# Two-layer hybrid encoder trunk: the residual in DRAM during the mixers, and the value products of a scan step after the step before it

## The chip, the cores and the metric

The kernel runs on one core of one Trainium2 chip. The metric is the device time of one execution in microseconds (us). Matrix products run on TensorE (PE, with its weight loads as PEld), elementwise work on VectorE (DVE) and ScalarE (ACT); nearly all transfers are issued on the queue of SyncE (SP). GpSimd (POOL) only clears a few edges.

## What is computed

Two layers and a final RMS norm over 256 tokens of width 1024, in float32. The inner widths are 2816 (feed-forward) and 8 heads of 64 (mixers).

```python
for l in range(DEPTH):
    x = x + 0.5 * gt1 * swiglu(modulate(rmsnorm(x), sh1, sc1), wi[l, 0], wo[l, 0])
    h = modulate(rmsnorm(x), sh2, sc2)
    x = x + gt2 * hybrid_mixer(h)
    x = x + 0.5 * gt3 * swiglu(modulate(rmsnorm(x), sh3, sc3), wi[l, 1], wo[l, 1])
return rmsnorm(x, final_norm)

def hybrid_mixer(h):
    proj = h @ w_in
    o_a = dilated_attention(...)            # mixer A
    o_b = neighborhood_attention(...)       # mixer B
    o_c = rwkv7_bidirectional(...)          # mixer C, a scan over the tokens
    return (sigmoid(gz0) * (o_a @ P_a) + sigmoid(gz1) * (o_b @ P_b)
            + sigmoid(gz2) * (o_c @ P_c)) @ w_out

def _rwkv_step(state, inp):
    r, w, k, v, a_vec, b_vec = inp
    sa = einsum("dbhvk,dbhk->dbhv", state, a_vec)
    state = state * w[..., None, :] + sa[..., None] * b_vec[..., None, :] + v[..., None] * k[..., None, :]
    return state, einsum("dbhvk,dbhk->dbhv", state, r)
```

The shifts, scales and gates (`sh`, `sc`, `gt`) are nine products of the conditioning vector with `ada_w` per layer.

## The kernel before

Activations lie transposed, 128 channels by 256 tokens a tile. Every weight product is done in three matmuls on two fp32r halves of weight and activation (lines 404 to 406, `mm3`): these are the **dense** matmuls. Weights stream as 512 KB tiles `wraw` (three buffers, line 345); ACT casts a high half `whi` (line 360) and DVE subtracts it for the low half `wlo` (line 369).

**The planner.** The order of the instructions on each engine is fixed when the kernel is built. The code is written as threads (generators). `Order.run` steps the thread that can start first by a table of durations, and writes its instructions down. The thread `main` yields the dense products; the rest are spawned beside it. Memory is a counted resource: `take(s_big)` and `free_big` count the pool of big tiles (`big`, 4 KB per partition, `NBIG` buffers), `take(s_z)` the pool of small ones (`small`, `NZ`), `take(s_px)` and `take(s_pm)` the eight PSUM banks. A thread that finds no buffer stands still, and so does everything after it in that thread.

**The residual** `xT` (128 x 8 x 256) is a tile of its own that is held through the whole kernel. In a mixer it is read at the start (`modulated`, which makes the normed input `h`) and not again until `residual` adds the mixer's output.

**A mixer** (`mixer`, from line 853) runs its dense work by `ORDER = "cabAgB"`: projections for C, A and B, then the gates and branch product of A (`join(0)`), the gates of C (`gates2`, which takes two big tiles `sg2` first), `join(1)`, and last the branch product of C (`branch(2)`), which needs the finished scan, and `w_out`. 480 dense matmuls stand between the start of `gates2` and the branch product of C.

**The scan of C** goes over four chunks of 64 tokens, both directions at once. Chunk `n` needs:

- `invert` (line 1142, two threads that take the chunks in turn, at most `NCK` = 2 chunks in hand): products `pG`, masks on DVE, a block inverse in `blocks8` (one PE product `p` at line 1228, then a row of short DVE operations), and three doubling levels, each with a product `pX` (line 1181), a copy, a product `pT` (line 1193), a masked copy and a transpose (`flip`, line 1245) on DVE. The result is `TT`.
- `values` (line 1247): transposes `pBT` (line 1258), products `pvt` (line 1267) and `pMV` (line 1277) with their copies; they depend on the chunk but not on the state. The results are `bu`, `uv` and `W1`.
- `scan` (line 1285): `pAS`, `pU`, `pS`, `pY` in a row, each after the copy of the one before, from the state of chunk `n - 1`.

Before the change `invert` takes all tiles of a chunk at once, those of `values` too:

```python
for _ in range(5 - (n == 3) + (n == ns[0])):
    yield take(s_big)
```

`post` normalizes the scan's output (products `pvar` and `pgi`, line 1402 and 1420) and writes `oC`, the input of the last branch product. Beside all this, `ada` reads the `ada_w` blocks (`araw`, 512 KB each, line 495) and reduces each on DVE (line 468) with the lowest priority; every one needs a big tile too.

Of the kernel before, what the change touches and what calls it, by code (L numbers as in the profile page):

```python
# [21 lines left out]
BIG = 1e30  # L22
TWO_PI_PARTS = (6.28125, 0.0019350051879882812, 3.0199159819e-07)
ROUND = 12582912.0
NBIG, NZ, NZ2 = 34, 10, 2
NRAW, NSPL, NADA, NPM = 3, 4, 2, 3
ORDER = "cabAgB"
NCK, NLR = 2, 2
WARM = 0
NJ0 = 8  # L30
NXF, NXM = 4, 8
# [130 lines left out]
def wait(ev):  # L162
    return ("wait", ev, 0, 0)
# [28 lines left out]
def trunk(ctx, tc, A, out):  # L192
# [36 lines left out]
        eng.dma_start(t, A[key])  # L229
        return t  # L230

    xT = act.tile([128, KT, S], F32, name="xT")
    csb = const.tile([128, D], F32, name="csb")
    cT = cload("cT", [128, KT], eng=nc.sync)
    ident = cload("ident", [128, 128], eng=nc.sync)
# [393 lines left out]
    def modulated(l, n, st, ha):  # L629
        yield from rstd(st)  # L630
        yield wait(st.e_A)
        for k in range(KT):
            yield take(s_z)
            t = small("ht")
            yield on("DVE", 0.4)
            V.scalar_tensor_tensor(t, xT[:, k], st.Ac[:, k:k + 1], st.r, op0=OP.mult, op1=OP.mult)
            od.spawn(mod_put(l, n, k, t, ha), 1)
        st.used()
# [214 lines left out]
    def mixer(l, st):  # L853
        yield take(s_big, 4)
        ha = Act("h", KT)
        od.spawn(modulated(l, 1, st, ha), 0)
        vec = tmp.tile([128, 14, 4], F32, name="vec", bufs=1)
        mul = tmp.tile([128, 2], F32, name="mul", bufs=1)
        for t, src in ((vec[:, 0:13], "vec"), (mul, "mul")):
# [262 lines left out]

        e_inv, e_val = ([Event() for _ in range(4)] for _ in range(2))
        CH = {}
        s_ck = Sem(NCK)
        n_inv, e_got = [0], [Event() for _ in range(5)]

        def toks(c):
            return slice(c * 64, c * 64 + 64)
# [1 line left out]
        def invert(ns):  # L1131
            for e in e_ab:
                yield wait(e)
            for n in ns:
                cs = (n, 3 - n)
                if n > 0:
                    yield wait(e_got[n - 1])
                yield take(s_ck)
                for _ in range(5 - (n == 3) + (n == ns[0])):
                    yield take(s_big)  # L1140
                od.set(e_got[n])
                if n == ns[0]:
                    tx = big("tx", (128, 2, 2, 4, 64))
                    T, X = tx[:, 0], tx[:, 1]
                G = [big("G", (128, 2, 4, 128)) for _ in range(2)]
                uv = big("uv", (128, 2, 8, 64))
                bu = big("bu", (128, 2, 8, 64)) if n < 3 else None
                tw = big("tw", (128, 2, 2, 4, 64))
                TT, W1 = tw[:, 0], tw[:, 1]
                for d in range(2):  # L1150
                    yield take(s_px, 2)
                    pp = [paux("pG", (128, 4, 128)) for _ in range(2)]
                    yield on("PE", 1.3)
                    for i in range(4):
                        for b in range(2):
                            hs = half(b)
                            P.matmul(pp[b][:, i], BK[d][i // 2][hs, i % 2, cs[d]].rearrange("p a b -> p (a b)"),
                                     ar_view(d, i // 2)[hs, :, i % 2, toks(cs[d])], start=True, stop=True)
                    for b in range(2):
                        yield on("DVE", 0.6)  # L1160
                        V.tensor_mul(G[b][:, d], pp[b], mg[:, d][:, None, :].to_broadcast([128, 4, 128]))
                        od.release(s_px)
                yield from blocks8(G, X, TT)
                yield on("DVE", 0.6)
                flip(T, TT)
                od.spawn(values(n, cs, G, bu, uv, W1), VPRIO)
                for lv in range(3):
                    w = 8 << lv

                    def part_(t, d, a):  # L1170
                        return t[:, d].rearrange("p h c -> p (h c)").rearrange("p (x a s) -> p x a s", a=2, s=w)[:, :, a]

                    def halves_(t, a):
                        return skew(part_(t, 0, a), part_(t, 1, 1 - a))

                    yield take(s_px)
                    px = paux("pX", (128, 2, 4, 64))
                    yield on("PE", 0.85)
                    for d in range(2):
                        for h in range(8):  # L1180
                            P.matmul(px[half(h), d, h // 2], G[h % 2][half(h), d, h // 2, 0:64], T[half(h), d, h // 2],  # L1181
                                     start=True, stop=True)
                    if lv == 0:
                        yield from copy_any(X, px, 512)
                    else:
                        yield from copy_any(halves_(X, 0), halves_(px, 0), 256)
                    od.release(s_px)
                    yield take(s_px)
                    pt = paux("pT", (128, 2, 4, 64))
                    yield on("PE", 0.85)  # L1190
                    for d in range(2):
                        for h in range(8):
                            P.matmul(pt[half(h), d, h // 2], X[half(h), d, h // 2], TT[half(h), d, h // 2], start=True, stop=True)  # L1193
                    yield on("DVE", 0.335)
                    V.copy_predicated(halves_(TT, 1), lvl[:, lv].rearrange("p d (x s) -> p d x s", s=w), halves_(pt, 1))
                    od.release(s_px)
                    if lv < 2:
                        yield on("DVE", 0.6)
                        flip(T, TT)
                CH[n] = (G, bu, uv, TT, W1)  # L1200
                yield wait(e_val[n])
                od.set(e_inv[n])
            n_inv[0] += 1
            free_big(1 if n_inv[0] == 1 else 5)

        def blocks8(G, m, TT):

# [36 lines left out]

            V.transpose(t.rearrange("p d a b -> p (d a b)"), tt.rearrange("p d a b -> p (d a b)"))

        def values(n, cs, G, bu, uv, W1):
            for d in range(2):
                yield wait(e_rkv[d, 2])
            if n < 3:  # L1250
                yield take(s_px, 2)
                p = [paux("pBT", (128, 2, 4, 64)) for _ in range(2)]
# [26 lines left out]
            yield from copy_any(W1, p, 512)  # L1279
            od.release(s_px)  # L1280
            od.set(e_val[n])

        e_y = {(d, t): Event() for d in range(2) for t in range(2)}

        def scan():
# [2 lines left out]
            yield take(s_big)  # L1288
            for n in range(4):
                cs = (n, 3 - n)  # L1290
                yield wait(e_inv[n])
                G, bu, uv, TT, W1 = CH[n]
                ar = lambda d, h, z: ar_view(d, h // 4)[half(h), z, h // 2 % 2, toks(cs[d])]
# [52 lines left out]
                od.release(s_px)  # L1346
                free_big(5 - (n == 3))
                od.release(s_ck)
                ST = sn
            free_big(5)  # L1350

# [382 lines left out]
        ha.free()  # L1734
        yield take(s_big, 4)
        ma = Act("m", KT)
        yield wait(e_oC)
        yield from branch(2, oC[0], gts)
        free_big(4)
# [2 lines left out]
        yield wait(have[l, 5])  # L1742
        yield on("DVE", 0.07)
        V.tensor_scalar(g, mod(l, 5), 0.5, None, op0=OP.mult)
        p3 = []
        for m in range(NPM):
            yield take(s_pm)
# [23 lines left out]
    def main():  # L1771
# [14 lines left out]
        for k in range(KT):  # L1786
            yield on("DVE", 0.34)
            V.tensor_mul(xT[:, k], xT[:, k], st.r)
            if k % 2 == 0 or k == KT - 1:
                k0 = max(k - 1, 0) if k < KT - 1 else k  # L1790
                nc.sync.dma_start(out[:, k0:k + 1], xT[:, k0:k + 1])

    od.spawn(main(), 7, True)
# [124 lines left out]
```

## Time and profile before

| | us |
|---|---|
| median of 3 runs | 1579.02 (1576.25 to 1579.44) |
| profiled execution, device time | 1579.55 |
| its span, first to last instruction | 1577.7 |
| PE busy / PE weight loads busy | 1509.2 / 1440.4 |
| DVE busy / ACT busy | 1288.8 / 856.1 |
| mean granted PE clock | 0.98 |

The profile is one execution on the chip. A share of busy time is a mean over stages. The table by stretches gives the busy time of each engine in a piece of the span, and the granted PE clock there; a timeline gives single instructions, with the idle time of the engine before each in brackets and what ended it. The two mixers run from about 220 to 585 us and from about 1000 to 1355 us.

### The profile page before, as it was taken

How to read it: one execution, taken by the hardware profiler on the slowest of the kernel's cores; microseconds unless marked ns; L12 is line 12 of the kernel's file. 1: busy time of each engine (PE TensorE's matmuls, PEld its weight loads, DVE VectorE, ACT ScalarE, POOL GpSimd, SP SyncE). 2: the span in 40 equal slices, each digit the busy share in tenths (PEclk: the TensorE clock that was granted, in tenths of full speed). 3: DMA queues.
4: the chain of work that ended last, by engine and by line, in shares of the span. 5: the costliest groups of instructions: out<-in, count | busy, mean ns of one | idle time of the engine just before them, and what ended most of it. 6: DMA issues, size and time to landing. Idle time of an engine off the chain costs nothing.

```text
span 1577.7 us, 36363 instructions
## 1 busy us (share of the span) xinstructions
PE 1509.2 (96%) x14470; PEld 1440.4 (91%) x14470; DVE 1288.8 (82%) x2732; ACT 856.1 (54%) x1730; POOL 2.3 (0%) x22
## 2 busy tenths in 40 slices
PE   6999999999899989999999999999999987999997
PEld 6998999979689879999999999998888977999997
DVE  8888789989768688988789877999897687998664
ACT  4556457566344347555565545676654433665554
POOL 0000000000000000000000000000000000000000
PEclk9999999999899969999999999999999988999999
DMA  9687864446223435887668885543652352457553
GB/s 345 215 301 269 277 224 162 163 147 234 100 95 133 135 139 196 274 289 262 221 208 278 276 273 195 189 159 129 219 165 100 122 190 106 146 202 267 188 187 121
DMA packets 96226, 311.58 MB, mean 197 GB/s; under 512 B 11444, under 2 KB 22964, under 8 KB 96056
## 3 DMA queue, kind: packets, MB, share of 16 engines
q1 hardware_dynamic: 95768, 309.15, 57.8%
q8 instruction: 113, 1.85, 0.5%
q14 instruction: 57, 0.47, 0.1%
q10 hardware_dynamic: 288, 0.10, 0.0%
HBM read 308.17 MB, written 1.05 MB: 196 GB/s over the span
## 4 chain that ended last, share of the span: by engine, by line
PE 88%; DVE 6%; DMA 3%; issue 1%; ACT 1%; SPq 1%; DVEq 0%; ACTq 0%
PE pmain L404 21%; PE pmain L405 20%; PE pmain L406 20%; DMA araw<-in_ada_w_dram 3%; PE pearly L404 2%; PE pearly L406 2%; PE pearly L405 2%; PE pX L1181 1%; DVE araw L468 1%; PE pT L1193 1%; PE pS L1499 1%; PE pfirst L405 1%; PE pfirst L406 1%; PE pfirst L404 1%; DVE wlo L369 1%
## 5 line engine op out<-in xcount | busy, mean ns | idle before, releaser
L360 ACT CAST whi<-wraw 128x512 fp32r<-128x512 f32 x828 | 508.5, 619 | 444.6 <-PE pmain L405 291.8
L369 DVE TENSOR_TENSOR wlo<-wraw,whi 128x512 fp32r<-128x512 f32 x828 | 566.6, 689 | 118.0 <-ACT whi L360 108.0
L404 PE MATMUL pmain<-h,whi 128*128 128x256 f32 x1840 | 528.1, 287 | 0.0
L405 PE MATMUL pmain<-h,whi 128*128 128x256 f32 x1840 | 517.4, 281 | 0.0
L406 PE MATMUL pmain<-h,wlo 128*128 128x256 f32 x1840 | 515.6, 280 | 0.0
L404 PEld LDWEIGHTS pmain<-h,whi 128*128 128x128 f32 x1840 | 346.1, 188 | 12.2 <-issue 8.2
L406 PEld LDWEIGHTS pmain<-h,wlo 128*128 128x128 f32 x1840 | 347.4, 189 | 0.3 <-DVE wlo L369 0.2
L405 PEld LDWEIGHTS pmain<-h,whi 128*128 128x128 f32 x1840 | 346.4, 188 | 1.1 <-issue 0.7
L468 DVE CUSTOM_DVE_ANT_0 araw<-araw,csb 128x1024 f32<-128x1024 f32 x144 | 174.7, 1218 | 47.1 <-DMA araw<-in_ada_w_dram 46.9
L406 PE MATMUL pmain<-z,wlo 128*128 128x256 f32 x704 | 198.5, 282 | 7.0 <-DVE wlo L369 7.0
L405 PE MATMUL pmain<-z,whi 128*128 128x256 f32 x704 | 198.4, 282 | 0.0
L404 PE MATMUL pmain<-z,whi 128*128 128x256 f32 x704 | 197.7, 281 | 0.0
L406 PEld LDWEIGHTS pmain<-z,wlo 128*128 128x128 f32 x704 | 132.8, 189 | 8.5 <-DVE wlo L369 8.4
L404 PEld LDWEIGHTS pmain<-z,whi 128*128 128x128 f32 x704 | 132.7, 189 | 0.0
L405 PEld LDWEIGHTS pmain<-z,whi 128*128 128x128 f32 x704 | 132.7, 188 | 0.0
L404 PE MATMUL pearly<-xh,whi 128*128 128x258 f32 x320 | 91.5, 286 | 0.0
L406 PE MATMUL pearly<-xh,wlo 128*128 128x258 f32 x320 | 90.4, 283 | 0.0
L405 PE MATMUL pearly<-xl,whi 128*128 128x258 f32 x320 | 90.1, 282 | 0.0
L405 PEld LDWEIGHTS pearly<-xl,whi 128*128 128x128 f32 x320 | 60.6, 189 | 0.0
L404 PEld LDWEIGHTS pearly<-xh,whi 128*128 128x128 f32 x320 | 60.6, 189 | 0.0
L406 PEld LDWEIGHTS pearly<-xh,wlo 128*128 128x128 f32 x320 | 60.4, 189 | 0.0
L427 ACT CAST z<-ffz 128x256 fp32r<-128x256 f32 x76 | 30.6, 405 | 35.2 <-DVE ffz L659 34.8
(301 smaller groups left out, 2369.8 us busy)
## 6 DMA issues: line engine op xcount, KB each, us to landing
wraw<-in_ffn_wi_dram SPq DMA_DIRECT2D x160, 512.0 KB, 4.6
araw<-in_ada_w_dram SPq DMA_DIRECT2D x144, 512.0 KB, 6.4
wraw<-in_ffn_wo_dram SPq DMA_DIRECT2D x88, 512.0 KB, 4.6
wraw<-in_w_in_dram SPq DMA_DIRECT2D x78, 512.0 KB, 4.0
wraw<-in_w_gb_dram SPq DMA_DIRECT2D x72, 512.0 KB, 3.8
w0raw<-in_ffn_wi_dram SPq DMA_DIRECT2D x16, 512.0 KB, 11.1
wraw<-in_w_out_dram SPq DMA_DIRECT2D x16, 512.0 KB, 3.7
bt<-in_bt_dram SPq DMA_DIRECT2D x16, 192.0 KB, 4.7
```

What stands on the lines that cost most here:

```text
L360: S_.copy(hi, part(q))
L369: V.tensor_tensor(lo, part(q), hi, op=OP.subtract)
L404: P.matmul(o, w[0], xh, start=first, stop=False)
L405: P.matmul(o, w[0], xl, start=False, stop=False)
L406: P.matmul(o, w[1], xh, start=False, stop=last)
L427: S_.copy(self.hi(k), src)
L468: V.tensor_tensor_reduce(out=raw, in0=raw, in1=csb, scale=0.5, scalar=0.0, op0=OP.mult, op1=OP.add, accum_out=modT[l][:, blk:blk + 1])
L1181: P.matmul(px[half(h), d, h // 2], G[h % 2][half(h), d, h // 2, 0:64], T[half(h), d, h // 2], start=True, stop=True)
L1193: P.matmul(pt[half(h), d, h // 2], X[half(h), d, h // 2], TT[half(h), d, h // 2], start=True, stop=True)
L1499: P.matmul(pS[e][:, t], qT[half(e), hp, t * 128:(t + 1) * 128], kT[half(e), hp], start=True, stop=True)
```

## The change

- The residual becomes two big tiles of the pool (`Residual`). In each mixer, once the normed input is made, both halves are stored to a DRAM tensor `xs` and their two buffers go to the pool (`norm`); after the last buffers for `w_out`'s input are taken, two buffers are taken again and the halves are loaded (`restore`). The thread of the dense products waits for that load before `w_out`.
- The big pool has 36 buffers, and 34 are counted while the residual lies in it. The small pool has 8 buffers instead of 10.
- `invert` takes three big tiles for a chunk (four the first time). `values` takes the other two itself, and only when the scan has released `s_vl` (one chunk in hand), at the end of the step before. `scan` waits for `values` by itself, and `invert` no longer waits for it.
- The output leaves in pairs that do not cross the two tiles.

```diff
-NBIG, NZ, NZ2 = 34, 10, 2
+NBIG, NZ, NZ2 = 36, 8, 2
-NCK, NLR = 2, 2
+NCK, NLR, NVL = 2, 2, 1
...
-    xT = act.tile([128, KT, S], F32, name="xT")
+    class Residual:
+        def __init__(self):
+            s_big.n -= 2
+            self.t = [big("xT") for _ in range(2)]
...
+    xT = Residual()
+    xs = [nc.dram_tensor(f"xs{l}", (128, KT, S), F32, kind="Internal").ap() for l in range(L)]
...
-        od.spawn(modulated(l, 1, st, ha), 0)
+        e_x = Event()
+        def norm():
+            yield from modulated(l, 1, st, ha)
+            for q in range(2):
+                yield on("SP", 1.45, 2.5)
+                nc.sync.dma_start(xs[l][:, 4 * q:4 * q + 4], xT.t[q])
+            xT.t = None
+            free_big(2)
+        def restore():
+            for _ in range(2):
+                yield take(s_big)
+            xT.t = [big("xT") for _ in range(2)]
+            for q in range(2):
+                yield on("SP", 1.45, 2.5)
+                nc.sync.dma_start(xT.t[q], xs[l][:, 4 * q:4 * q + 4])
+            od.set(e_x)
+        od.spawn(norm(), 0)
...
-        s_ck = Sem(NCK)
-        n_inv, e_got = [0], [Event() for _ in range(5)]
+        s_ck, s_vl = Sem(NCK), Sem(NVL)
+        n_inv, n_val, e_got, e_vgot = [0], [0], *([Event() for _ in range(5)] for _ in range(2))
...
-                for _ in range(5 - (n == 3) + (n == ns[0])):
+                for _ in range(3 + (n == ns[0])):
                     yield take(s_big)
...
-                uv = big("uv", (128, 2, 8, 64))
-                bu = big("bu", (128, 2, 8, 64)) if n < 3 else None
...
-                od.spawn(values(n, cs, G, bu, uv, W1), VPRIO)
+                od.spawn(values(n, cs, G, TT, W1), VPRIO)
...
-                CH[n] = (G, bu, uv, TT, W1)
-                yield wait(e_val[n])
                 od.set(e_inv[n])
-            n_inv[0] += 1
-            free_big(1 if n_inv[0] == 1 else 5)
+            free_big()
...
-        def values(n, cs, G, bu, uv, W1):
+        def values(n, cs, G, TT, W1):
             for d in range(2):
                 yield wait(e_rkv[d, 2])
+            if n > 0:
+                yield wait(e_vgot[n - 1])
+            yield take(s_vl)
+            for _ in range(1 + (n < 3)):
+                yield take(s_big)
+            od.set(e_vgot[n])
+            uv = big("uv", (128, 2, 8, 64))
+            bu = big("bu", (128, 2, 8, 64)) if n < 3 else None
+            CH[n] = (G, bu, uv, TT, W1)
...
+            n_val[0] += 1
+            if n_val[0] == 4:
+                free_big(4)
...
                 cs = (n, 3 - n)
+                yield wait(e_val[n])
                 yield wait(e_inv[n])
...
                 od.release(s_ck)
+                od.release(s_vl)
...
         ma = Act("m", KT)
+        od.spawn(restore(), 0)
...
+        yield wait(e_x)
         p3 = []
...
-            if k % 2 == 0 or k == KT - 1:
-                k0 = max(k - 1, 0) if k < KT - 1 else k
+            if k % 2 == 1 or k > 5:
+                k0 = k - 1 if k < 6 else k
```

**How the order moves.** On PE the feed-forward stages and the first half of each mixer stand in the same order; what moves lies in the second half of each mixer, from the first product `pG` on. Below, `pmain<-h`, `pmain<-o` and `pmain<-oC` are dense products; `x16` is a row of equal instructions.

Layer 0, PE, at the start of `gates2` (its dense products are `pmain<-h`). Before:

```order
L1181 MATMUL pX<-tx,G 64x64 x16
L1258 MATMUL pBT<-c_ident,bk 128x64 x16
L1193 MATMUL pT<-tw,tx 64x64 x16
L1530 MATMUL pPT<-c_ident,prob 128x128 x8
L1181 MATMUL pX<-tx,G 64x64 x16
L1539 MATMUL po<-prob,vv 64x256 x4
L1193 MATMUL pT<-tw,tx 64x64 x16
L404 MATMUL pmain<-h,whi 128x256
L405 MATMUL pmain<-h,whi 128x256
L406 MATMUL pmain<-h,wlo 128x256
```

The same place in the changed kernel (its lines 418 to 420 are the dense ones, 1213 is `pX`, 1296 `pBT`, 1225 `pT`):

```order
L420 MATMUL pmain<-h,wlo 128x256
L1213 MATMUL pX<-tx,G 64x64 x16
L1296 MATMUL pBT<-c_ident,bk 128x64 x16
L1225 MATMUL pT<-tw,tx 64x64 x16
L418 MATMUL pmain<-h,whi 128x256
L419 MATMUL pmain<-h,whi 128x256
```

Before, no dense product of `gates2` stands ahead of the second `pT`; now 39 dense matmuls of `gates2` stand ahead of the first `pX`, and the two inversions lie among them. In layer 1 the changed order still has a stretch without a dense product at that place: six `pX` and five `pT` groups (two chunks), two heads' `pS`, `pPT` and `po`, and four pairs of `pbon` products; before the change three `pX` and three `pT` groups of one chunk, its first scan step and eight pairs of `pbon` products stood there.

Layer 1, PE, at the end of the dense work that does not need the scan. Before, after the last `pmain<-o` of `join(1)` come 27 rows of scan work without a dense product, of which the last are:

```order
L1337 MATMUL pY<-G,uv 64x64 x16
L1341 MATMUL pY<-ar,st 64x64 x16
L1277 MATMUL pMV<-uv,G 64x64 x16
L1302 MATMUL pAS<-st,ar 64x64 x16
L1310 MATMUL pU<-tw 64x64 x16
L1337 MATMUL pY<-G,uv 64x64 x16
L1341 MATMUL pY<-ar,st 64x64 x16
L1402 MATMUL pvar<-c_sel,gsq 128x2 x8
L1420 MATMUL pgi<-c_ident,gsq 128x128 x8
L404 MATMUL pmain<-oC,whi 128x256
L405 MATMUL pmain<-oC,whi 128x256
```

The last `pY` (lines 1379 and 1383) of the changed kernel:

```order
L420 MATMUL pmain<-o,wlo 128x256
L1379 MATMUL pY<-G,uv 64x64 x16
L1383 MATMUL pY<-ar,st 64x64 x16
L418 MATMUL pmain<-o,whi 128x256
L419 MATMUL pmain<-o,whi 128x256
L420 MATMUL pmain<-o,wlo 128x256
```

It now lies among the dense products of `join(1)`, 114 dense matmuls ahead of the first `pmain<-oC`, and the last `pgi` 36 ahead of it. In layer 0, whose end looked alike before (15 dense matmuls after the last but one `pS`, then two `pY` steps, `pvar` and `pgi` without a dense product), the last `pY` stands 78 ahead and the last four `pgi` directly ahead of it.

SP's queue at the end of layer 0's mixer, changed kernel (line 359 is `wraw`, 887 the load of the residual):

```order
L359 DMA wraw<-in_w_gb_dram 128x1024 x5
L887 DMA xT<-xs 128x1024
L359 DMA wraw<-in_w_gb_dram 128x1024
L359 DMA wraw<-in_w_out_dram 128x1024
L887 DMA xT<-xs 128x1024
L359 DMA wraw<-in_w_out_dram 128x1024 x7
```

The loads stand ahead of the second to eighth `w_out` tiles, and the buffers that they fill were last read over 200 dense matmuls earlier. The second is issued about six dense matmuls after the last branch product begins, some 138 ahead of the first `residual`. The stores stand at the start of the mixer, between `w_in` tiles; the buffers that they free are next written over 360 dense matmuls later. The `araw` transfers that stood in one burst of 8 (layer 0) and 12 (layer 1) at the end of the mixer are spread over its second half; in layer 1 seven of them stand in one row at the start of `gates2`.

## Rows read from the trace of the kernel before

**Rows 1.** The page's first part: span, and busy time of each engine.

```profile
span 1577.7 us, 36363 instructions
...
PE 1509.2 (96%) x14470; PEld 1440.4 (91%) x14470; DVE 1288.8 (82%) x2732; ACT 856.1 (54%) x1730; POOL 2.3 (0%) x22
```

**Rows 2.** Stretches of both mixers: length, busy PE, PEld, DVE, ACT, POOL; clock, DMA.

```profile
391.58:426.36 34.78, 27.55 (x292) 21.54 (x291) 28.61 (x77) 12.84 (x33) 0.00 (x0) 0.85 0.37 124
426.36:544.90 118.54, 116.48 (x1899) 108.17 (x1895) 84.76 (x183) 50.30 (x96) 0.00 (x0) 1.00 0.33 108
544.90:576.30 31.40, 20.69 (x242) 18.61 (x242) 22.77 (x50) 8.18 (x18) 0.00 (x0) 0.62 0.40 151
1142.92:1176.20 33.28, 33.28 (x283) 29.66 (x282) 31.68 (x79) 19.63 (x48) 0.00 (x0) 1.00 0.43 144
1176.20:1196.59 20.39, 15.98 (x394) 14.21 (x392) 12.64 (x23) 5.99 (x12) 0.00 (x0) 1.00 0.42 140
1196.59:1290.90 94.31, 93.41 (x1087) 85.84 (x1086) 71.67 (x158) 45.47 (x97) 0.00 (x0) 1.00 0.37 124
1290.90:1347.50 56.60, 41.45 (x864) 36.60 (x863) 43.18 (x103) 15.58 (x32) 0.00 (x0) 0.79 0.37 141
```

**Rows 3.** Timeline of PE, layer 0's block inverse: start, length, instruction, [idle before].

```profile
407.05 2.08 PE L1228 MATMUL p<-tx,c_b 128*128 128x512 f32 x2 [5.21 <-DVE tx L1222]
```

**Rows 4.** Timeline of PE, the end of layer 0's mixer.

```profile
554.23 2.58 PE L1337 MATMUL pY<-G,uv 128*64 128x64 f32 x32 [3.57 <-DVE uv L1312]
...
569.71 0.58 PE L404 MATMUL pmain<-oC,whi 128*128 128x256 f32 x1 [3.73 <-ACT oC L1447]
...
577.32 0.28 PE L404 MATMUL pmain<-oC,whi 128*128 128x256 f32 x1
577.44 0.28 PE L405 MATMUL pmain<-oC,whi 128*128 128x256 f32 x1
```

**Rows 5.** Timeline of DVE, the same end: an `araw` reduction that waits.

```profile
552.35 1.22 DVE L468 CUSTOM_DVE_ANT_0 araw<-araw,csb 128x1024 f32<-128x1024 f32 x1 [2.81 <-DMA araw<-in_ada_w_dram]
...
554.10 1.21 DVE L468 CUSTOM_DVE_ANT_0 araw<-araw,csb 128x1024 f32<-128x1024 f32 x1
...
555.24 1.21 DVE L468 CUSTOM_DVE_ANT_0 araw<-araw,csb 128x1024 f32<-128x1024 f32 x1
```

**Rows 6.** Stretches again, the `araw` reductions alone: length, DVE busy (count), clock, DMA.

```profile
1176.20:1196.59 20.39, 1.23 (x1) 1.00 0.42 140
1290.90:1342.15 51.25, 15.58 (x13) 0.82 0.41 155
```

**Rows 7.** Timeline of PE, the end of layer 1's mixer.

```profile
1338.77 1.97 PE L1420 MATMUL pgi<-c_ident,gsq 128*128 128x128 f32 x8 [0.84 <-DVE gsq L1415]
1342.15 0.58 PE L404 MATMUL pmain<-oC,whi 128*128 128x256 f32 x1 [1.41 <-ACT oC L1447]
```

**Rows 8.** DMA issues of two tiles: KB each, median us from issue to landing.

```profile
araw<-in_ada_w_dram SPq DMA_DIRECT2D x144, 512.0 KB, 6.4
...
wraw<-in_w_out_dram SPq DMA_DIRECT2D x16, 512.0 KB, 3.7
```

**Rows 9.** ACT, copies of `values`, table load: busy us, mean ns | idle before.

```profile
L849 ACT COPY uv<-pvt 64x512 f32<-64x512 f32 x16 | 9.3, 580 | 9.7 <-PE pvt L1267 9.5
...
L1409 ACT ACT_TABLE_LOAD x4 | 5.1, 1283 | 0.1
...
L849 ACT COPY tw<-pMV 128x512 f32<-128x512 f32 x8 | 4.7, 586 | 8.1 <-PE pMV L1277 6.8 <-DMA wraw<-in_w_gb_dram 1.2
```

**Rows 10.** Timeline of PE, layer 1, a scan step among dense products.

```profile
1255.20 1.15 PE L1302 MATMUL pAS<-st,ar 64*64 64x64 f32 x32
...
1257.87 1.15 PE L1310 MATMUL pU<-tw 64*64 64x64 f32 x32
...
1261.28 1.15 PE L1322 MATMUL pS<-uv,bu 128*64 128x64 f32 x32
```

More of the change, by code (lines that the diff above doesn't have):

```diff
@@ L230, in cload, with __getitem__ @@
         return t
-    xT = act.tile([128, KT, S], F32, name="xT")
+    class Residual:
+        def __init__(self):
+            s_big.n -= 2
+            self.t = [big("xT") for _ in range(2)]
+        def __getitem__(self, key):
+            k = key[1]
+            if isinstance(k, slice):
+                return self.t[k.start // 4][:, k.start % 4:(k.stop - 1) % 4 + 1]
+            return self.t[k // 4][:, k % 4]
+    xT = Residual()
+    xs = [nc.dram_tensor(f"xs{l}", (128, KT, S), F32, kind="Internal").ap() for l in range(L)]
     csb = const.tile([128, D], F32, name="csb")
```

## The prediction

> **What bounds the kernel now.** I read the page's first part first. PE is busy for 1509.2 of 1577.7 us [rows 1]; no other engine is near, so time can come only from the places where PE has nothing to do, and what the others do matters only where PE waits for it. The table by stretches says where those places are. [Rows 2] cuts the second half of both mixers at the points where the dense products stop and start again, and the reader is to compare length with busy PE, and to look at the clock in the column behind POOL:
>
> - start of `gates2`, layer 0 (391.58 to 426.36): 34.78 − 27.55 = 7.23 us idle, clock 0.85;
> - end of the mixer, layer 0 (544.90 to 576.30): 10.71 us idle, clock 0.62;
> - start of `gates2`, layer 1 (1176.20 to 1196.59): 4.41 us idle, clock 1.00;
> - end of the mixer, layer 1 (1290.90 to 1347.50): 15.15 us idle, clock 0.79.
>
> The two stretches between them, filled with dense products, idle 2.06 of 118.54 and 0.90 of 94.31 us. So the same scan work costs PE next to nothing where dense products stand around it, and much where they don't.
>
> The clock is a second loss. Granted 0.62 means that part of the stretch ran at the lower of the two levels (1.2 of 2.4 GHz) after PE had idled. The loss is (1 − clock) times busy PE at least and times the whole stretch at most: 4.1 to 5.2 us, 7.9 to 11.9 us, none, and 8.7 to 11.9 us. Idle and clock together: 11.3 to 12.4, 18.6 to 22.6, 4.4 and 23.9 to 27.0 us, in all **58 to 66 us**. That is all the change can earn.
>
> The timeline then says what is waited for. At the ends PE waits for the copies of the scan's chain (`uv` on DVE 3.57 us, then `oC` on ACT 3.73 us) [rows 4]; in layer 1 for `gsq` and `oC` [rows 7]. At the start of `gates2` it waits 5.21 us for DVE's row of short operations in `blocks8` [rows 3], with the dense products standing behind: `gates2` needs two big tiles, which the inversions held. A lack of buffers set that order, not a lack of work.
>
> **The ends of the mixers.** The last `pY` stands now 78 (layer 0) and 114 (layer 1) dense matmuls ahead of the last branch product. A dense matmul follows the one before at 0.12 us (the last two of [rows 4]). In layer 1 the last `pgi` has 36 behind it, 36 × 0.12 = 4.3 us; from the start of `pgi` to the first product of `oC` it took 1342.15 − 1338.77 = 3.38 us [rows 7]. So the wait is covered and the whole stretch's loss goes: **+23.9 to 27.0**. In layer 0 four `pgi` stand directly ahead, so part of the 3.73 us stays, on which I put 2.5: **+16.1 to 20.1**. The cover is thin: if the scan is late by more than 78 × 0.12 = 9.4 us, the end waits again.
>
> **The starts of `gates2`.** In layer 0, 39 dense matmuls now go ahead of the first `pX`. But the wait for `p` hangs on DVE; `pG` and a head's `pS` come ahead of it, about 1.1 us each (like the other rows of 32 small matmuls, 1.15 [rows 10]), so 5.2 shrinks to about 3, and the clock will fall again after it. I let 8 of the 11.3 to 12.4 us stay: **+3.3 to 4.4**. In layer 1 the gap remains in the order, and with two inversions in it in place of one. Besides, seven `araw` reductions stand there in one row; each keeps DVE for 1.14 us (the last two of [rows 5]), 8 us in all, where one ran before [rows 6], and in the 33.28 us ahead DVE is busy for 31.68 already [rows 2]. I double the loss to 9: **−4.6**.
>
> **What is interleaved.** The PE work that ran without dense products comes between them. The two filled stretches lose 2.96 of 212.85 us, 1.4%; of the 45.6 us of PE work that I count as moving, **−0.6**.
>
> **`araw`.** 10 and 13 of these reductions ran in the ends ([rows 6] for layer 1), where DVE was half idle. They move into the second half of the mixer. A reduction whose tile is late holds up DVE's queue and everything behind it: 2.81 us once [rows 5]. The ends hid it; among dense products it hits PE only if it stands in the scan's chain. I take half of two such waits: **−2.8**. DVE as a whole has room: 136.14 us of work in layer 0's three stretches and 127.49 in layer 1's last three, over 184.72 and 171.30 us less 20 each, is 83% and 84%.
>
> **The residual's transfers.** Eight of 512 KB, 3.7 to 6.4 us from issue to landing [rows 8]. The stores' buffers are next written over 360 dense matmuls (43 us) later; the second load goes out some 138 dense matmuls (16 us) ahead of the first `residual`; the slots it fills were last read over 200 earlier. The queues have room (DMA share 0.33 to 0.44 [rows 2]). Hidden, so 0. Without that cover: one landing a layer in front of `w_out`, 13 us. The loads are issued ahead of seven `w_out` tiles on SP's queue; a wait for a buffer there would hold these up, hence the point on when the slots were last read. The regrouped output moves nothing on PE: 0.
>
> **Small edits.** With 8 small buffers the feed-forward order on PE stays as it was, 0, at worst some 2 us. The order has eight more table loads on ACT, 8 × 1.283 = 10.3 us [rows 9]; ACT is busy for 45.47 of 94.31 us in the filled stretch [rows 2]. Hidden, 0.
>
> **Sum.** From 23.9 + 16.1 + 3.3 − 4.6 − 0.6 − 2.8 = 35.3 to 27.0 + 20.1 + 4.4 − 4.6 − 0.6 − 2.8 = 43.5; middle 39.4. The profiled execution has 1579.55, so 1540.1; the median of the runs lies 0.5 below the profiled time, so **1539.6 us**.
>
> **A rule against the busy share of PE.** [Rows 2] gives PE 348.84 of 389.30 us busy in the seven stretches, 40.5 us free, and 314.63 for the weight loads, 74.7 us free. I worked with the first. The Trainium skill, "Perfetto Trace Analysis", section "Identifying the Most-Contended Engine", calls the time in which matmuls are busy a bad measure, since they are pipelined, and the share of weight loads a good one. By that rule 74.7 us could be filled, and the best case would be 1579.55 − 74.7 − 0.5 = 1504. The trace speaks against it here: in the stretch from 426.36, full of work, loads take 108.17 us beside 116.48 of matmuls, and the remaining 10.4 us were not filled.
>
> **The rivals.**
>
> *DVE becomes the bound* (0.20). The dense products are ahead, but the scan's chain and two inversions, side by side, fill DVE's queue, and PE waits in the middle of the mixer. For it: [rows 3], the 31.68 of 33.28 us, and the seven reductions in a row. Against it: the mean of 83%. Price: one more front per layer like the old ones, 11.9 + 4.4 = 16.3 us given back; 1539.6 + 16.3 = 1556.
>
> *The fronts go too* (0.12). The dense products cover the inversions as in the filled stretches; the gain is the whole 58 us: 1579.5 − 58 = 1521. For it: 39 dense matmuls are 4.7 us of cover. Against it: layer 1's order.
>
> *Slower: `values` comes onto the scan's path* (0.05). Before, a chunk's `values` ran while the step before was still going on; now it starts when that step has ended. A step then has three more products at 1.15 us at most [rows 10] and five copies of 0.58 [rows 9] in its chain, 6.35 us, for three steps in two layers 38 us. If none is covered and the clock follows as in [rows 2] (11.3 lost for 7.23 idle, times 1.57), that is 60 us: 1539.6 + 60 = 1600. It turns slower where idle in these steps passes 39.4 / 1.57 = 25 us, 4.2 a step. Against it: the scan step of [rows 10] ran among dense products with no idle ahead of its products, and the changed order has 9 to 18 dense matmuls (1 to 2 us) between the products of such a handover.
>
> *The change doesn't do what it says* (0.03). The scan is late as before, by DVE and ACT, and only the place of the wait changes: 1579, give or take 3.
>
> **How the numbers follow.** Forecast 0.60, the rivals 0.20, 0.12, 0.05 and 0.03. The likeliest gives 1540. The range runs from a little below the case without fronts (1521) to a little above the DVE case (1556): **1518 to 1560**; outside lie the slower case, that without effect, and their neighbours. A measurement of this kernel tells about 0.2% (3.2 us) from no change. Faster by more: 0.60 + 0.20 + 0.12 = 0.92; within: 0.03; slower: 0.05.
>
> **What would show it.** In the profile after: no stretch of over 3 us without PE work between the last `pY` and the product of `oC` in layer 1, and a clock of 0.95 or more there; layer 0's end with one wait for `oC` of 1 to 4 us; at the start of `gates2` a remaining idle of about 3 us ahead of `p` in layer 0, and more than 4.41 us idle in layer 1, released by DVE; busy PE within 10 us of 1509 less what the slow clock had stretched. Wrong would be: idle ahead of `pAS` or `pU` released by the copies of `pBT`, `pvt` or `pMV` (the slower rival), idle ahead of `w_out` or `residual` released by a DMA of `xT`, or DVE over 90% busy through the second half (the first rival).

## The result and the profile after

| | before | after |
|---|---|---|
| median, us | 1578.42 (4 runs, 1576.25 to 1579.44) | 1554.78 (4 runs, 1552.96 to 1554.94) |
| span of the profiled execution, us | 1577.7 | 1553.1 |
| mean granted PE clock | 0.98 | 0.98 |

The ratio is 0.9849, 95% interval 0.9832 to 0.9866: faster by 24 us, inside the range (1518 to 1560) and 15 us short of the forecast of 1540.

The page's first part, after, answers to [rows 1]:

```profile
span 1553.1 us, 36366 instructions
...
PE 1508.4 (97%) x14470; PEld 1438.6 (93%) x14470; DVE 1282.1 (83%) x2724; ACT 870.0 (56%) x1746; POOL 2.4 (0%) x22
```

PE has the same instructions and is busy for as long as before, though in the mixers much less of its time ran at the slow clock. Of the 24.6 us that the span lost 23.8 are idle time; what the slow clock gave back was spent on something else.

The table by stretches (columns as in [rows 2]), after, cut at the same products as before: from the place where the two orders begin to differ (in layer 1 a little ahead of it) to about the first product of `oC`, and from there to the first of `w_out`.

```profile
1129.99:1316.80 186.81, 180.02 (x2602) 162.40 (x2601) 151.69 (x347) 91.69 (x193) 0.00 (x0) 0.97 0.44 144
1316.80:1332.50 15.70, 14.56 (x95) 14.16 (x96) 12.35 (x30) 7.05 (x14) 0.00 (x0) 0.78 0.50 172
392.62:555.51 162.89, 155.09 (x2402) 138.50 (x2400) 128.89 (x290) 74.07 (x148) 0.00 (x0) 0.98 0.39 131
555.51:572.01 16.50, 14.73 (x96) 14.07 (x97) 13.92 (x34) 7.23 (x15) 0.00 (x0) 0.79 0.42 137
```

The same two pairs of stretches before:

```profile
391.58:569.71 178.13, 158.24 (x2402) 142.59 (x2401) 132.30 (x299) 69.29 (x141) 0.00 (x0) 0.92 0.36 123
569.71:584.74 15.03, 14.92 (x97) 14.17 (x97) 12.12 (x30) 7.07 (x14) 0.00 (x0) 0.78 0.23 76
...
1142.92:1342.15 199.23, 178.89 (x2602) 161.84 (x2601) 155.55 (x351) 84.87 (x185) 0.00 (x0) 0.95 0.40 137
1342.15:1357.00 14.85, 14.72 (x99) 13.98 (x100) 12.62 (x31) 7.17 (x15) 0.00 (x0) 0.81 0.26 83
```

The clock of these long stretches is a mean over idle and busy time. What it costs PE is read from the pieces in which the clock was 0.50, by PE's busy time there. Before:

```profile
405.79:416.03 10.24, 8.98 (x32) 5.89 (x34) 8.77 (x32) 1.68 (x3) 0.00 (x0) 0.50 0.53 198
552.57:576.46 23.89, 16.54 (x114) 14.81 (x115) 18.12 (x41) 7.08 (x15) 0.00 (x0) 0.50 0.32 130
1293.26:1303.50 10.24, 7.10 (x96) 5.32 (x98) 9.57 (x30) 1.66 (x3) 0.00 (x0) 0.50 1.01 381
1330.81:1334.22 3.41, 3.22 (x54) 3.10 (x56) 0.00 (x0) 0.14 (x1) 0.00 (x0) 0.50 0.00 0
1337.63:1347.87 10.24, 7.87 (x31) 6.64 (x32) 7.32 (x20) 3.22 (x9) 0.00 (x0) 0.50 0.01 2
```

After:

```profile
406.71:413.54 6.83, 4.47 (x20) 2.78 (x21) 6.80 (x24) 2.90 (x11) 0.00 (x0) 0.50 0.72 277
556.90:563.72 6.82, 6.05 (x25) 5.59 (x26) 4.38 (x13) 2.05 (x5) 0.00 (x0) 0.50 0.47 154
1171.30:1178.12 6.82, 6.43 (x77) 5.50 (x77) 5.71 (x15) 0.59 (x2) 0.00 (x0) 0.50 0.91 321
1239.56:1242.98 3.42, 3.42 (x41) 3.08 (x36) 0.39 (x1) 0.59 (x1) 0.00 (x0) 0.50 0.69 273
1318.07:1324.90 6.83, 6.27 (x29) 5.91 (x28) 4.02 (x10) 2.45 (x5) 0.00 (x0) 0.50 0.46 160
```

| us | layer 0 | layer 1 |
|---|---|---|
| idle (length less busy PE), before → after | 20.0 → 9.6 | 20.5 → 7.9 |
| slow clock, half of PE's busy time at 0.50, before → after | 12.8 → 5.3 | 9.1 → 8.1 |
| so removed, by the sum of the two | 17.9 | 13.6 |
| shorter, from the same start to `w_out` | 13.8 | 11.3 |
| PE longer at its work | 4.1 | 2.3 |

Half is the most that the slow clock can have cost: the same 16 `pG` matmuls took 2.08 us at 0.50 and 1.16 at 1.00 (the last timeline of this document), a loss of 0.44. By 0.44 the last row is 3.2 and 2.1, so PE is 5.3 to 6.4 us longer at its work in the two layers together.

Two things are left to explain: why the last branch product still waits at a slow clock (0.79, 0.78), and why PE takes 5 to 6 us longer for the same instructions.

The timeline of PE at the end of layer 1's mixer, after, answers to [rows 7]:

```profile
1310.13 0.60 PE L1463 MATMUL pgi<-c_ident,gsq 128*128 128x128 f32 x4
...
1313.31 0.28 PE L420 MATMUL pmain<-h,wlo 128*128 128x256 f32 x1
1314.84 0.28 PE L418 MATMUL pmain<-oC,whi 128*128 128x256 f32 x1
1317.38 0.39 PE L419 MATMUL pmain<-oC,whi 128*128 128x256 f32 x1 [2.26 <-DVE oC L1492]
...
1318.82 0.58 PE L418 MATMUL pmain<-oC,whi 128*128 128x256 f32 x1 [0.56 <-ACT oC L1490]
```

And the timeline of DVE in the same microseconds (`wlo` is the cast of coming weights, `rkv` and `oC` are `post`, `sg` and `mgd` the branch before):

```profile
1313.77 0.68 DVE L383 TENSOR_TENSOR wlo<-wraw,whi 128x512 fp32r<-128x512 f32 x1
1314.37 0.41 DVE L1486 TENSOR_TENSOR rkv<-rkv,pgi 128x256 f32<-128x256 f32 x1
1314.70 0.68 DVE L383 TENSOR_TENSOR wlo<-wraw,whi 128x512 fp32r<-128x512 f32 x1
1315.31 0.41 DVE L1743 SCALAR_TENSOR_TENSOR sg<-sg,pmain 128x256 f32<-128x256 f32 x1
1315.64 0.68 DVE L383 TENSOR_TENSOR wlo<-wraw,whi 128x512 fp32r<-128x512 f32 x1
1316.24 0.41 DVE L1747 TENSOR_TENSOR mgd<-mgd,sg 128x256 f32<-128x256 f32 x1
1316.57 0.41 DVE L1488 TENSOR_TENSOR rkv<-rkv,bon 128x256 f32<-128x256 f32 x1
1316.91 0.41 DVE L1492 TENSOR_TENSOR oC<-rkv,oC 128x256 fp32r<-128x256 f32 x1
```

The first product of `oC` comes without a wait, as forecast. But a branch product goes through four tiles of `oC`, and the later ones are still in DVE's queue, which has no gap here and in which casts of weights stand between `post`'s operations. From the last `pgi` to the last tile some 9 us pass (1310.13 to 1319.2), not 3.38. The short idle is followed by products at the slow clock.

### The profile page after: what moved, and what is told of

It reads as the page before. It is cut to its first block, busy times and chain, and to the rows that moved or that the text cites. A ratio compares the mean times of both kernels' runs of the same rounds, so it can differ in the third digit from the quotient of the medians.

```text
span 1553.1 us, 36366 instructions
## 1 busy us (share of the span) xinstructions
PE 1508.4 (97%) x14470; PEld 1438.6 (93%) x14470; DVE 1282.1 (83%) x2724; ACT 870.0 (56%) x1746; POOL 2.4 (0%) x22
## 4 chain that ended last, share of the span: by engine, by line
PE 89%; DMA 4%; DVE 4%; issue 1%; ACT 1%; SPq 0%; DVEq 0%; ACTq 0%
PE pmain L418 21%; PE pmain L419 20%; PE pmain L420 20%; DMA araw<-in_ada_w_dram 3%; PE pearly L418 3%; PE pearly L419 2%; PE pearly L420 2%; PE pT L1225 1%; PE pX L1213 1%; PE pG L1189 1%; DVE wlo L383 1%; PE pfirst L419 1%; PE po L1582 1%; PE pfirst L420 1%; PE pfirst L418 1%
## 5 line engine op out<-in xcount | busy, mean ns | idle before, releaser
L418 PEld LDWEIGHTS pmain<-h,whi 128*128 128x128 f32 x1840 | 346.8, 188 | 13.8 <-issue 8.7
## 6 DMA issues: line engine op xcount, KB each, us to landing
w0raw<-in_ffn_wi_dram SPq DMA_DIRECT2D x16, 512.0 KB, 10.9
```

What stands on the lines that cost most here:

```text
L418: P.matmul(o, w[0], xh, start=first, stop=False)
```

## The experiments

The table gives, from each trace, the time from the first product of the first branch to the first of `oC`, and from there to the first of `w_out` (layer 0 / layer 1). Ratios are to the kernel before, run on the same chip.

| run | median, us | ratio, 95% interval | to `oC`, us | `oC` to `w_out`, us |
|---|---|---|---|---|
| before | 1578.42 | 1 | 211.0 / 207.9 | 15.0 / 14.6 |
| after | 1554.78 | 0.9849 (0.9832 to 0.9866) | 195.7 / 193.5 | 16.5 / 17.7 |
| residual_only | 1576.52 | 0.9983 (0.9971 to 0.9996) | 211.1 / 205.3 | 11.4 / 14.7 |
| values_only | 1557.41 | 0.9871 (0.9843 to 0.9898) | 198.9 / 195.6 | 11.3 / 16.5 |
| short_araw | 1549.85 | 0.9821 (0.9802 to 0.9840) | 194.2 / 192.2 | 17.0 / 16.0 |
| no_sqrt_table | 1552.71 | 0.9839 (0.9820 to 0.9858) | 195.4 / 191.3 | 16.9 / 16.7 |
| post_first | 1546.31 | 0.9790 (0.9772 to 0.9808) | 194.0 / 191.1 | 15.9 / 11.5 |
| ada_early | 1550.16 | 0.9809 (0.9790 to 0.9829) | 201.8 / 199.5 | 11.2 / 10.9 |
| values_two | 1556.02 | 0.9852 (0.9833 to 0.9870) | 196.5 / 201.9 | 16.2 / 11.5 |
| post_pace8 | 1549.84 | 0.9820 (0.9799 to 0.9841) | 198.2 / 196.8 | 11.6 / 12.3 |
| post_pace6 | 1552.31 | 0.9837 (0.9823 to 0.9852) | 200.9 / 198.4 | 11.3 / 11.2 |
| values_post | 1552.58 | 0.9843 (0.9827 to 0.9859) | 199.8 / 196.0 | 11.3 / 12.8 |

**The two parts alone.** *residual_only*: the changed kernel with `invert`, `values` and `scan` as before.

```diff
-                for _ in range(3 + (n == ns[0])):
+                for _ in range(5 - (n == 3) + (n == ns[0])):
...
-                yield wait(e_val[n])
                 yield wait(e_inv[n])
```

> Only the residual's part of the change: residual in DRAM, pools of 36 and 8, but the old invert, values and scan. In the order the end of layer 0's mixer now has 219 dense matmuls behind the last pgi (none before, none in the changed kernel), layer 1's end keeps some 6.5 us of scan work without a dense product (16.6 before), and both starts of gates2 keep theirs. My theory (each mixer's loss is what its stalls and the slow clock behind them cost, and hardly anything else): layer 0's end gives all of its 18.6 to 22.6 us, layer 1's some 10 of 24 to 27, so 1547 to 1553 us, no slower than the whole change. Rival (the values' part is what matters, buffers alone only move the stall): 1565 us or more.

1576.52 us: my theory fell, and the rival's time came out. Layer 0's end is covered (11.4 us), yet the time to `oC` is what it was. The table by stretches of this run (columns: busy PE, PEld, DVE, ACT, POOL, clock, DMA):

```profile
400.00:470.00 70.00, 56.40 (x835) 46.14 (x834) 62.16 (x151) 23.38 (x55) 0.00 (x0) 0.90 0.41 138
470.00:510.00 40.00, 34.06 (x655) 30.05 (x656) 29.90 (x66) 12.98 (x24) 0.00 (x0) 0.96 0.21 75
510.00:573.63 63.63, 63.63 (x870) 61.43 (x865) 39.45 (x78) 32.39 (x64) 0.00 (x0) 1.00 0.38 119
```

and of the kernel before:

```profile
400.00:470.00 70.00, 61.04 (x909) 52.49 (x908) 48.79 (x122) 28.65 (x65) 0.00 (x0) 0.93 0.31 102
470.00:510.00 40.00, 39.84 (x459) 36.96 (x458) 32.61 (x67) 18.15 (x33) 0.00 (x0) 1.00 0.36 118
510.00:569.71 59.71, 48.94 (x959) 45.59 (x958) 43.65 (x99) 19.98 (x39) 0.00 (x0) 0.86 0.43 153
```

The scan work ran earlier, in stretches where DVE was then busy for 62 of 70 us, and PE waited there: 13.6 + 5.9 us idle from 400 to 510 instead of 9.0 + 0.2, and none after, where 10.8 had been. Here a wait that was taken from the end came back in the middle, where the work met a full DVE.

*values_only*: the new `values`, `invert` and `scan` with the residual in SBUF.

```diff
-NBIG, NZ, NZ2 = 36, 8, 2
+NBIG, NZ, NZ2 = 34, 10, 2
...
-    xT = Residual()
+    xT = act.tile([128, KT, S], F32, name="xT")
```

> Only the values' part: values takes its buffers after the step before, scan waits for values, the residual stays in SBUF, pools of 34 and 10. In the order layer 0's end has 105 dense matmuls behind the last pgi, layer 1's end none behind pgi but 78 behind the last pY; both starts of gates2 keep their scan work without dense products; PE changes between dense and small products 85 and 86 times (66 and 64 before, 92 and 89 in the changed kernel). My theory: both ends gained, about 20 + 17 us, less 0.25 us for each of some 40 changes, 10 us: 1550 to 1556 us. Rival (the two buffers of the residual are needed as well): 1565 us or more. Rival that values on the scan's path costs time: idle ahead of pAS or pU of 4 us a step.

1557.41 us: this part alone brings nearly all of the gain, just above the expected span, its interval overlapping that of the whole change. The longest wait ahead of a scan product is 0.77 us (`pS`), so the slower rival's 4 us a step are not there.

**The end of the mixer.** *no_sqrt_table*:

```diff
-            S_.activation(r, p, AF.Sqrt, scale=1.0 / 64, bias=eps_g)
+            S_.activation(r, p, AF.Square, scale=1.0 / 64, bias=eps_g)
```

> The changed kernel in the same order, with a Square in place of the Sqrt of post (the scan's output is normalized by a wrong factor), so that ACT does not load a table between it and the gates' tanh: in the last 12 us of each mixer four loads of 1.28 us go from ACT's queue. My theory (these loads stand in the chain pvar, gr, pgi, oC, which the branch product waits for, 3.45 and 2.82 us idle and 3.4 us of slow clock a layer): gain 5 to 12 us, 1543 to 1550. Rival (DVE's queue, with the casts of the weights between post's operations, sets the end, and the loads are hidden): within 2 us of the changed kernel, 1553 to 1557.

The rival holds, though the time lies 0.3 us under its span: 1552.71 us, with an interval that overlaps the changed kernel's, and `oC` to `w_out` still takes 16.9 and 16.7. The edit took away 13 table loads of 1.28 us, all those of `post` and of the gates, so the loads on ACT are nearly all hidden.

*post_first*:

```diff
-                    od.spawn(post(d, t), 3)
+                    od.spawn(post(d, t), -2)
```

> The changed kernel with post (the scan's normalization, which writes oC) ahead of all else in the planner. In the order layer 1 now has 102 dense matmuls behind its last pgi (36 in the changed kernel), layer 0 has 9 (none). My theory (in layer 1 the branch product of C waits for post's row on DVE, which the casts of the weights lengthen; a longer cover takes that away): layer 1's branch product, 17.67 us from its first matmul to w_out's first, comes to 11 to 13, layer 0's stays at 15 to 17; 1548 to 1551 us. Rival (DVE is full in the second half, so that what is done earlier for post is done later for the others): within 2 us of the changed kernel.

1546.31 us, faster than both kernels and than my theory's span, with an interval apart from the changed kernel's. The two last branch products, table by stretches:

```profile
1310.34:1321.82 11.48, 11.48 (x99) 11.48 (x97) 11.10 (x26) 6.91 (x14) 0.00 (x0) 1.00 0.83 288
555.50:571.36 15.86, 13.64 (x97) 13.03 (x98) 13.69 (x34) 7.10 (x14) 0.00 (x0) 0.89 0.46 153
```

Layer 1, with 102 dense matmuls of cover, has no idle and the full clock; layer 0, with 9, waits as before. So an uncovered end costs 17.67 − 11.48 = 6.2 us in layer 1 of the changed kernel, and 16.5 − 11.5 = 5.0 in layer 0.

**DVE and `araw`.** *short_araw*:

```diff
-        V.tensor_tensor_reduce(out=raw, in0=raw, in1=csb, scale=0.5, scalar=0.0, op0=OP.mult, op1=OP.add,
+        n = 64 if blk // 8 in (5, 6, 7) else D
+        V.tensor_tensor_reduce(out=raw[:, 0:n], in0=raw[:, 0:n], in1=csb[:, 0:n], scale=0.5, scalar=0.0, op0=OP.mult, op1=OP.add,
```

> The changed kernel in the same order, where the araw reductions of the mixers (48 in all, 1.14 us each on DVE) run over 64 of their 1024 columns, so that three of the ada vectors of each layer are wrong sums; DVE gets back about 1 us each, 48 us, with all loads and buffers as they were. My theory (no reduction stands ahead of the wait for p in layer 0, and the waits at oC are ACT's table loads and post's own row on DVE): gain 2 to 6 us, 1549 to 1553. Rival (DVE as a whole is the bound of the second half, and araw in front of the scan's operations is what remains): gain 10 to 20 us, 1535 to 1545.

1549.85 us: 5 us for 43 us taken off DVE (1282.1 to 1238.8 us busy by the pages), as expected (the two intervals overlap a little). The order being the same, `araw` is no large part of what is left.

*ada_early*:

```diff
-PACE, START = 7, 110
+PACE, START = 8, 70
```

> The changed kernel with the loads of ada starting 70 us after the mixer's start, in steps of 8 us (110 and 7 in the changed kernel), so that more of the araw reductions lie in the mixer's first half and their buffers are free in the second. In the order both last branch products now have 105 and 141 dense matmuls behind the last pgi (0 and 36), and no stretch without a dense product has more than 3.3 us of scan work (11 in layer 1). My theory (the remaining losses are the two fronts and the two ends, and DVE's queue at those places): 1534 to 1546 us. Rival (as in the run with the residual alone, the wait moves to the middle of the mixer, where DVE is busy throughout): 1551 us or more.

1550.16 us, between the two. Both ends are covered (11.2, 10.9), but 6 us in each layer came back ahead of `oC`, as idle in front of `pX` and `p`, released by DVE, and as slow clock behind it. The ends are 5.3 and 6.8 us shorter, the stretches ahead of them 6.1 and 6.0 longer: within the second halves the rival's mechanism took all of the gain. The 4.6 us by the medians come from elsewhere, and no run shows from where.

*values_two* (`NVL = 2`):

> The changed kernel with two chunks' values in hand (NVL 2), so that values no longer waits for the step before. In the order layer 1 has 177 dense matmuls behind the last pgi (36 in the changed kernel) and 16 changes fewer between dense and small products; layer 0 is as it was. My theory: layer 1's end is covered, 5 to 6 us, and the fewer changes give 2 to 4: 1545 to 1550 us. Rival (the order of values is what brings the gain, by holding buffers back for the inversions): 1558 us or more.

1556.02 us, the same as the changed kernel: layer 1's end is covered (11.5), and 8.5 us came back ahead of it, with 6.81 us in one wait for `p` on DVE. My theory fell, and the rival's time did not come either: what a second chunk in hand wins at the end it loses ahead of it.

**A change between kinds.** *switch_cost*, a kernel of its own:

```python
for _ in range(24): group()
dense(288)
for _ in range(24): group(); dense(12)
for _ in range(12): group(); group(); dense(24)
for _ in range(48): group(); dense(6)
```

> A kernel of its own, which computes none of the reference's output: dense matmuls (128x128 weights, 256 columns, fp32r) and groups of 32 small ones (64x64, fp32) like pX, with nothing to wait for, on PE alone: 96 dense, 24 groups in a row, 288 dense in a row, then the same 24 groups and 288 dense taken in turn (12 dense and a group), then in pairs (24 dense and two groups), then 48 groups with 6 dense each. My theory (a change between the two kinds costs PE time, since the changed kernel's PE is about 11 us longer at work than its removed stalls say, with some 48 more changes): the turn by 12 takes 8 to 14 us longer than the two in a row, the pairs half of that, the turn by 6 twice. Rival (changes cost nothing, the 11 us lie in waits too short to see): all within 2 us of the sum of the two rows.

The table by stretches of PE alone (length, busy, clock, DMA), one row for each line of the code:

```profile
22.23:44.20 21.97, 21.97 (x750) 1.00 0.02 4
44.20:78.93 34.73, 34.73 (x290) 1.00 0.01 1
78.93:143.89 64.96, 64.96 (x1057) 1.00 0.01 2
143.89:204.85 60.96, 60.96 (x1057) 1.00 0.01 2
204.85:300.20 95.35, 95.35 (x1825) 1.00 0.01 2
```

The first row holds 748 small matmuls, 0.94 us for a group of 32 (the missing ones ran earlier), so 24 groups and 288 dense in rows take 22.6 + 34.7 = 57.3 us. In turn they take 64.96 (+7.7), in pairs 60.96 (+3.7), and 48 groups by 6 take 95.35 instead of 79.9 (+15.5). Each time that is **0.32 us for going to a small group and back**, 0.16 a change, with PE busy throughout and at the full clock, in one execution. The 7.7 us lie just under the expected 8 to 14.

**Towards a faster version.** *post_pace8* and *post_pace6* are post_first with `PACE` 8 and 6; *values_post* is values_only with `post` first.

> The run with post first, and ada's loads 8 us apart instead of 7. In the order both last branch products now have a cover behind the last pgi (81 and 45 dense matmuls; 9 and 102 in the run with post first). My theory (a cover of some 40 dense matmuls behind the last pgi is what a branch product of C needs): layer 0's branch product comes from 15.9 to 11 to 12.5 us, layer 1's stays below 12.5; the fronts stay; 1541 to 1545 us. Rival (what is gained at one place is lost in DVE's full stretches, as with the early ada loads): 1546 to 1550 us.

> The run with post first, and ada's loads 6 us apart. In the order both last branch products have a cover of over 100 dense matmuls behind the last pgi (114 and 126), and the longest stretch without dense products at the start of gates2 is 2.5 us in layer 0 and 10.6 in layer 1. My theory: both branch products 11 to 12 us, nothing more gained by the longer cover; 1541 to 1545 us. Rival (the scan that ends earlier meets a full DVE in the middle): 1546 to 1552 us.

> The values' part alone (the residual stays in SBUF, pools of 34 and 10) with post first, to see what the residual's two buffers are worth once the ends are covered (78 and 30 dense matmuls behind the last pgi). My theory (they are worth little: they shorten layer 0's front, and nothing else): 1545 to 1550 us, at most 4 above the run with post first (1546.3). Rival (they are needed, the end only hid it): 1552 us or more.

All three theories fell to their rivals: 1549.84, 1552.31 (0.3 us above its rival's span) and 1552.58 us. The first two cover both ends, and give it back ahead of `oC` (4 to 7 us a layer); the first can't be told from post_first, since the intervals overlap. The third shows that the residual's two buffers are worth something after all, 6 us by the medians beside post_first, and it lies ahead of `oC` (5.8 and 4.9 us a layer, less what layer 0's end gains); without `post` first the difference (1557.41 against 1554.78) could not be told from none.

## Why the prediction was right, and 15 us too low

The places of the gain were forecast rightly, but that 1554.78 lies in the range is partly luck: its upper end was drawn around a rival whose mechanism did not come true in this kernel. Two terms of the sum were mis-sized.

*The ends of the mixers, +23.9 to 27.0 and +16.1 to 20.1.* The mechanism was right: the stretches without dense products are gone, and the last `pY` is no longer waited for. The size failed at "36 × 0.12 = 4.3 us; from the start of `pgi` to the first product of `oC` it took 3.38 us. So the wait is covered". 3.38 us was the price of the first of four tiles with nothing but `post` in DVE's queue; beside dense work the same queue holds casts of weights, and the last tile comes 9 us after `pgi`. The ends kept 5.0 and 6.2 us where I had left 2.5 and 0: **8.7 us**.

*The interleaving, −0.6.* I took it from the idle share of the filled stretches (1.4%), but its cost is no idle time: PE counts as busy. (The 45.6 us of moved work in that term stand in no row.) PE was 5.3 to 6.4 us longer at its work: **4.7 to 5.8 us** too little. By the order the second halves have 92 and 89 changes between dense and small products instead of 66 and 64, 51 more. At the 0.16 us of switch_cost that would be 8.2 us, more than there is; here it comes to 0.10 to 0.13 a change, if all of it is changes. That changes cost PE time is shown, by switch_cost; that they are the whole of these 5 to 6 us is argued, and why a change is cheaper here than there stays open. Taken at the mean clock of the long stretches, the slow clock of before comes out too large (15.9 and 11.7 us instead of 12.8 and 9.1), and PE's longer work with it: the "about 11 us" in the expectation of switch_cost. Together the two terms make 13.4 to 14.5 us, where 39.4 − 24.6 = 14.8 were missing.

*The starts of `gates2`, 8 and 9 us left.* Right. The table by stretches, after:

```profile
400.00:425.00 25.00, 18.93 (x121) 13.48 (x119) 24.34 (x70) 11.44 (x31) 0.00 (x0) 0.86 0.37 127
...
1165.00:1190.00 25.00, 20.26 (x360) 17.81 (x358) 23.55 (x66) 10.15 (x30) 0.00 (x0) 0.86 0.67 228
```

6.07 us idle and at most 4.47 / 2 = 2.2 us of clock make 8.3 in layer 0, 4.74 + 6.43 / 2 = 8.0 in layer 1, with DVE busy for 24.34 and 23.55 of 25 us: it is DVE that these fronts wait for. In layer 0 the profile puts the longest wait down to "issue", but the tile that `p` reads leaves DVE's queue 0.1 us earlier:

```profile
408.28 0.69 DVE L1251 TENSOR_TENSOR tx<-w,c_d 128x512 f32<-128x512 f32 x1
...
409.07 2.04 PE L1257 MATMUL p<-tx,c_b 128*128 128x512 f32 x2 [4.46 <-issue]
```

So the wait for `p` kept 4.46 of its 5.21 us, where I had left about 3.

*`araw`, −2.8.* Not measured by itself. Taking most of the reductions' work away gave about 5 us, but the loads, and with them the waits for a late tile, stayed as they were.

*The transfers and small edits, 0.* In the trace after no engine waits for a load of `xT` from `xs`, and the table loads cost at most 2 us (no_sqrt_table, not told from none). The highest DMA share in [rows 2] is 0.43, not 0.44; nothing hangs on it.

*The rivals.* The time is that of "DVE becomes the bound" (1556), but not by its mechanism in the changed kernel: DVE is busy for 79 and 81% of the second halves up to `oC`, under the 90% that I had named. DVE bounds only the fronts and the ends. In residual_only, ada_early and values_two the rival's mechanism does appear, as waits for DVE in the middle of the mixer. The slower rival and the one without effect are out. Nor did the fronts go. By the rule of the Trainium skill ("Perfetto Trace Analysis", section "Identifying the Most-Contended Engine") that the busy share of weight loads tells the headroom of PE, 74.7 us were to be had by my estimate; the best run took 33 (ratio 0.979), and no run shows whether the rest can be had. switch_cost shows what a part of such time is: in turns of 12 the weight loads are busy for 60.16 of 64.96 us although PE waits for nothing, and the same work in two rows takes 57.3. There the headroom is the price of the changes.

*What I had named as signs.* From the last `pY` to the product of `oC` in layer 1 PE has no idle time and the clock is 1.00, as named, but it is 0.78 behind it. Layer 0's end has two waits for `oC`, 1.69 and 1.43 us, where I had named one. Layer 1's front idles 4.74 us, over 4.41, released by DVE, as named. PE's busy time did not fall by what the slow clock had stretched. The clock behind `oC` and PE's busy time point to the two terms that failed; none of the signs of being wrong is there.

## What to carry to other kernels

A chain that ends in several tiles is covered only when its last tile is, so take its length from the queue it will share later, not from the empty one in the trace of before. Work moved from a stall into dense work costs PE something for each change of kind, although no idle time shows it; keep small groups together. And a wait taken away at the end came back further ahead, in five of the runs here, mostly as waits for DVE: look at what the work will wait for in the stretch into which it moves, before counting the gain.

## What was not expected

The price of a change between dense and small products, 0.16 us in a kernel of its own, was in none of the rows that I had read of before. The other thing is the clock: it fell once while PE was busy without a gap. The table by stretches of the changed kernel, layer 1:

```profile
1230.00:1235.00 5.00, 5.00 (x88) 4.73 (x88) 4.25 (x11) 2.62 (x7) 0.00 (x0) 1.00 0.63 227
1235.00:1240.00 5.00, 5.00 (x67) 4.61 (x67) 3.48 (x10) 3.10 (x6) 0.00 (x0) 0.96 0.52 157
1240.00:1245.00 5.00, 5.00 (x58) 4.49 (x54) 2.29 (x4) 1.21 (x2) 0.00 (x0) 0.70 0.41 161
```

and the timeline of PE there:

```profile
1235.22 1.16 PE L1189 MATMUL pG<-ar,bk 64*128 64x128 f32 x16
...
1239.01 1.54 PE L1213 MATMUL pX<-tx,G 64*64 64x64 f32 x32
1240.48 2.08 PE L1189 MATMUL pG<-ar,bk 64*128 64x128 f32 x16
```

`pG` took 1.16 us and then 2.08 for the same 16 matmuls. What stood ahead were `pG`, 16 `pvar` products with two columns each, and few dense ones. Whether these low products made the clock fall was not tried.
